# Giving z the 512-column products of q and k, and its silu in two parts

## The chip, the cores and the metric

The kernel runs on one core of one Trainium2 chip. The metric is the device time of one execution in microseconds (us), as the median of three runs. Below, PE is the matmul engine (TensorE), PEld its weight loads, DVE is VectorE, ACT is ScalarE, POOL is GpSimd, and SP is the engine that issues the large loads.

## What is computed

One layer of a hybrid decoder on 256 tokens of width 1024: a SwiGLU block, then a mixer with two branches side by side (a Mamba-2 state-space branch, "SSD", and differential attention), then a second SwiGLU block, each with a normalisation before and after. The part that matters here is the mixer's input projection and what hangs on its output `z`:

```python
u = rmsnorm(h, mix_pre_g[l])
z, xbc, dt_raw, q, k, v, gate_logits = jnp.split(u @ w_in[l], IN_SPLITS, axis=-1)
...
y = ssd_chunked(xh, dt, a_head, bm, cm)                      # the state-space recurrence, by chunks of 128
y = (y + d_skip[:, None] * xh)
y = y.reshape(b, L, SSD_D_INNER) * jax.nn.silu(z)            # z: 256 tokens x 2048
y = rmsnorm(y.reshape(b, L, SSD_GROUPS, ...), 1.0) * norm_g
return y @ w_branch
```

z has 2048 columns and q and k have 1024 each. Everything is float32, and the result has to be close to float32.

## The kernel before

**Products in parts.** Every weight and every activation is split into a high and a low float32r part (`whi`/`wlo`, and `uh`/`ul` for the normalised input u), and a product is the sum of high x high, high x low and low x high. The weights come as chunks of 1 MB: SP loads a chunk into one of three `raw` buffers, ACT casts its halves to `whi` (L250), and DVE subtracts to get `wlo` (L253). `take()` hands out the next chunk and first splits the chunks up to three ahead, so that two casts and two subtractions go with every chunk.

**Two ways of multiplying a chunk of 256 weight columns** with all 256 tokens, over eight blocks of 128 in the contraction:

- `mm_t` (L294) makes 48 products of 256 columns: per half of the chunk (`m`), 8 times `whi` x `uh` (L301), 8 times `whi` x `ul` (L302) and 8 times `wlo` x `uh` (L304). All three kinds add up in the same place, so that one buffer of PSUM holds both halves of the chunk. The weights `whi` are loaded twice.
- `mm_w` (L306) makes 32 products: per half, 8 products of `whi` with `uh` and `ul` side by side, 512 columns wide (L316), and 8 of `wlo` x `uh`, 256 columns wide (L315, L318). A half fills a whole buffer: its first 256 columns hold the part with `uh` and its last 256 the part with `ul`. ACT copies the second part to SBUF (L320, or L323 with a scale) and DVE adds the first (L321, or L324).

In both, the buffers are those of the pool `pj`, of which there are three. The kernel before uses `mm_w` for the gate and up products of both SwiGLU blocks and for q and k, and `mm_t` for the convolution's inputs (xs, B and C) and for z.

**The stage around the change.** After the eight chunks of xs come eight chunks of z (L1326 to L1332): each takes its weights, multiplies with `mm_t`, and ACT copies the 512 columns of the buffer to `sz` (L1331). After z follow q and k, alternately, in four chunks each: q0, k0, q1, k1, and so on.

**Work in the background.** `back.run(us)` stands behind every chunk. It issues steps of a background queue worth so many planned microseconds: `BG_US` = 3.15 behind a chunk of z and `QK_US` = 2.4 behind one of q or k. The queue holds `ssd_work` for four groups of eight heads. A group transposes xs (PE `px`, L1061; DVE multiplies to `X`, L1062), builds four decay tiles `E` (ACT L362 and DVE L1078 write parts, ACT takes the exponential, DVE multiplies by `cbm`, L1083), multiplies them (32 products into `py`, L1093) and adds to xs (DVE, L1100). The products begin with the group's last E. Behind it comes `ssd_norm`, which multiplies xs by silu(z) (DVE, L1107), squares, and normalises.

**silu(z).** After the last chunk of z, `act_table(SILU)` loads ACT's table for silu, four activations of 1024 columns apply silu to `sz`, and `act_table(EXP_LN)` loads the table of exponential and logarithm again. Only then is `ssd_norm` put in the queue. `act_table` also keeps activations on their side of the load.

**Order.** In this stage the order of instructions on each engine is the framework's: it plans them when the kernel is built, and the chip keeps each engine's order to the letter. A wait of one instruction holds up all that stand behind it on that engine. From the gates on (`pgt`), PE's order is as written.

Of the kernel before, what the change touches and what calls it, by code (L numbers as in the profile page):

```python
# [18 lines left out]
AF = mybir.ActivationFunctionType  # L19
# [4 lines left out]
EXP_LN = "natural_log_exp_and_others"  # L24
# [16 lines left out]
WARM = 3  # L41
FILL = 2
TAIL = 3
BG_US = 3.15
QK_US = 2.4
GATE_US = 1.75
SSD_US = 1.55
DOWN = {"f1": "p q1 p p q2 p ppp", "f2": "q1 p q2 p q3 ppp"}
# [5 lines left out]
def tile_hybrid_layer(ctx: ExitStack, tc: tile.TileContext, x, ffn1_pre_g, ffn1_w_gate, ffn1_w_up,  # L54
# [4 lines left out]
    nc = tc.nc  # L59
# [5 lines left out]
    def k4(shape, name, dt=F32):  # L65
        return sb.tile(shape, dt, tag="k4", name=name, bufs=K4_BUFS)
# [4 lines left out]
    def k2(shape, name, dt=F32):  # L71
        return sb.tile(shape, dt, tag="k2", name=name, bufs=K2_BUFS)
# [7 lines left out]
    def pj(name):  # L80

        return ps.tile([P, 512], F32, tag="pj", name=name, bufs=3)

    def pjt(name):

        return pj(name).rearrange("p (m t) -> p m t", m=2)

    def bg(shape, name):
        return ps.tile(shape, F32, tag="bg", name=name, bufs=5)
# [3 lines left out]
    class Quad:  # L93
# [32 lines left out]
        def split(self, p):  # L126
            load_to(self.i + 2)
            hi = k4([P, 2, 512], f"wqh{self.i}{p}", F32R)
            src = self.quarter(self.PLAIN[p], p) if p in self.PLAIN else self.sum_of(p)
            nc.scalar.copy(hi, src)  # L130
            for later in self.products[self.products.index(p) + 1:][:1]:
                if later in self.SUMS:
                    self.sum_of(later)
            lo = k4([P, 2, 512], f"wql{self.i}{p}", F32R)
            last_lo[0] = nc.vector.tensor_sub(lo, src, hi.bitcast(F32)).ins
            self.give_back()
            return lambda kt: hi[:, kt, :], lambda kt: lo[:, kt, :]
# [121 lines left out]
    def split_to(n):  # L259

        while len(splits) < min(n, len(units)):
            of, p = units[len(splits)]
            if p is not None:
                splits.append(of.split(p))
                continue
            for _ in split_steps():
                pass

    def ahead_of(i, n):

        n *= 4
        while n > 0 and i < len(units):
            n -= 4 if units[i][1] is None else 1
            i += 1
        return i

    def take(ahead=AHEAD):

        i = taken[0]
        taken[0] += 1  # L280
        split_to(ahead_of(i, ahead))
        (of, p), w = units[i], splits[i]
        splits[i] = None
        if p is not None:
            return w
        his, los = w
        nj = chunks[of][1][1] // 2
        return (lambda j: his[j // nj][:, j % nj, :], lambda j: los[j // nj][:, j % nj, :])
# [5 lines left out]
    def mm_t(acc, w, act, k0=0, first=True, last=True, ks=range(KD)):  # L294

        (wh, wl), (ah, al, _) = w, act
        acc = acc if isinstance(acc, list) else [acc[:, m, :] for m in range(2)]
        for m in range(2):
            cs = slice(m * P, (m + 1) * P)
            for j in ks:  # L300
                nc.tensor.matmul(acc[m], wh(j)[:, cs], ah(k0 + j), start=first and j == ks[0], stop=False)  # L301
                nc.tensor.matmul(acc[m], wh(j)[:, cs], al(k0 + j), start=False, stop=False)  # L302
            for j in ks:
                nc.tensor.matmul(acc[m], wl(j)[:, cs], ah(k0 + j), start=False, stop=last and j == ks[-1])  # L304

    def mm_w(dst, name, w, act, scale=None):  # L306


        (wh, wl), (ah, _, ahl) = w, act
        for m in range(2):  # L310
            acc = pj(f"{name}{m}")
            cs = slice(m * P, (m + 1) * P)
            for j in range(KD):
                if j:
                    nc.tensor.matmul(acc[:, :T], wl(j)[:, cs], ah(j), start=False, stop=False)  # L315
                nc.tensor.matmul(acc, wh(j)[:, cs], ahl(j), start=j == 0, stop=j == KD - 1)  # L316
                if not j:
                    nc.tensor.matmul(acc[:, :T], wl(j)[:, cs], ah(j), start=False, stop=False)  # L318
            if scale is None:
                nc.scalar.copy(dst[:, m, :], acc[:, T:])  # L320
                nc.vector.tensor_tensor(dst[:, m, :], acc[:, :T], dst[:, m, :], ALU.add)  # L321
            else:
                nc.scalar.activation(dst[:, m, :], acc[:, T:], AF.Copy, scale=scale)  # L323
                nc.vector.scalar_tensor_tensor(dst[:, m, :], acc[:, :T], scale, dst[:, m, :], ALU.mult, ALU.add)  # L324
# [29 lines left out]
    def act_table(name):  # L354
        f = nc.scalar.preload_act_table_set(name)
        for prev in act_since:
            tc.add_manual_dep(f.ins, prev, order, reason="activation table")
        act_since.clear()
        act_fence[0] = f.ins.name

    def act(*args, **kw):
        a = nc.scalar.activation(*args, **kw)  # L362
        if act_fence[0] is not None:
            tc.add_manual_dep(a.ins, act_fence[0], order, reason="activation table")
        act_since.append(a.ins.name)
# [65 lines left out]
    def new_u(tag):  # L431
        for i in range(2):
            uT[i] = sb.tile([P, 4, 2, T], F32R, tag="u8", name=f"u{i}_{tag}", bufs=2)

    act_u = (lambda j: uT[j // 4][:, j % 4, 0, :], lambda j: uT[j // 4][:, j % 4, 1, :],
             lambda j: uT[j // 4][:, j % 4, :, :])
# [594 lines left out]
    for i in range(4):  # L1031
        acc = pjt(f"pbc{i}")
# [18 lines left out]
    sz = [None] * 4  # L1051
# [52 lines left out]
    def ssd_norm(groups):  # L1104

        def one(g):
            nc.vector.tensor_tensor(xs[g], xs[g], sz[g], ALU.mult)  # L1107
            sq = k4([P, 4, T], f"sqy{g}")
            nc.scalar.activation(sq, xs[g], AF.Square)
            yield 1.2  # L1110
            nc.vector.tensor_tensor(sq[:, 0:2, :], sq[:, 0:2, :], sq[:, 2:4, :], ALU.add)
            nc.vector.tensor_tensor(sq[:, 0, :], sq[:, 0, :], sq[:, 1, :], ALU.add)
            ssum = k2([P, 2, T], f"ssum{g}", F32R)
            split(ssum[:, 0, :], ssum[:, 1, :], sq[:, 0, :])
            yield 1.5
            yield BREAK
            pn = bg([P, T], f"pn{g}")
            for i in range(2):
                nc.tensor.matmul(pn, ones_r, ssum[:, i, :], start=i == 0, stop=i == 1)
            rs = sq[:, 1, :]  # L1120
            act(rs, pn, AF.Ln, scale=1.0 / 512, bias=eps_c)
            act(rs, rs, AF.Exp, scale=-0.5)
            yield 0.1
            for c in range(4):
                n = col["ng"] + g * 4 + c
                nc.vector.scalar_tensor_tensor(xs[g][:, c, :], xs[g][:, c, :], cols_a[:, n:n + 1], rs,
                                               ALU.mult, ALU.mult)
            yh[g] = k4([P, 4, T], f"yh{g}", F32R)
            yl[g] = k4([P, 4, T], f"yl{g}", F32R)
            split(yh[g], yl[g], xs[g])  # L1130
            xs[g] = sz[g] = None
            yield 2.8

        todo = [one(g) for g in groups]
        under_way = []
        while todo or under_way:
            if todo and len(under_way) < 2:
                under_way.append(todo.pop(0))
            for w in list(under_way):
                us = next(w, None)  # L1140
                if us is None:
                    under_way.remove(w)
                else:
                    yield us
# [170 lines left out]
    back = Background()  # L1315
    back.add(cb_work())
    for g in range(4):
        xs[g] = k4([P, 4, T], f"xs{g}")
        for i in range(2):
            acc = pjt(f"pxs{g}{i}")  # L1320
# [5 lines left out]
    for g in range(4):  # L1326
        sz[g] = k4([P, 4, T], f"sz{g}")
        for i in range(2):
            acc = pjt(f"pz{g}{i}")
            mm_t(acc, take(), act_u)  # L1330
            nc.scalar.copy(sz[g][:, i * 2:i * 2 + 2, :], acc)  # L1331
            back.run(BG_US)  # L1332
    act_table(SILU)
    for g in range(4):
        act(sz[g], sz[g], AF.Silu)
    act_table(EXP_LN)
    back.add(ssd_norm(range(4)))
    for c in range(4):
        if c % 2 == 0:
            qT[c // 2] = k4([P, 4, T], f"q{c}")  # L1340
            kT[c // 2] = k4([P, 4, T], f"k{c}")
        o = (c % 2) * 2
        mm_w(qT[c // 2][:, o:o + 2, :], f"pq{c}", take(), act_u, 0.125)
        back.run(QK_US)
        mm_w(kT[c // 2][:, o:o + 2, :], f"pk{c}", take(), act_u)
        back.run(QK_US)

# [81 lines left out]
    acc = [[bg([P, 512], f"acc_mx{b}{q}") for q in range(2)] for b in range(2)]  # L1429
# [47 lines left out]
```

## Time and profile before

| what | value |
| --- | --- |
| median of 3 runs | 738.33 us (738.31 to 738.46) |
| the profiled execution | 737.54 us, of which its span is 735.8 us |
| PE busy | 726.4 us (99%), 4211 products |
| DVE busy | 591.9 us (80%) |
| ACT busy | 462.1 us (63%) |
| granted clock of PE | 0.997 of full speed |

Times in the profile's rows are counted from the span's start. A row of the timeline gives the start, the duration, the engine, the line, the operation, what is written and read, its shape, how many instructions are merged, and in brackets how long the engine sat idle before it and for whom. PE's products overlap: what a product costs is the distance from its start to the start of the next, not its own duration.

### The profile page before, as it was taken

To read this page: it belongs to the slowest core of one execution; us is meant where nothing else is said; L and a number is where in the kernel's file an instruction comes from. 1 tells how busy PE (TensorE), PEld (TensorE's weight loads), DVE (VectorE), ACT (ScalarE), POOL (GpSimd) and SP (SyncE) were. 2 spreads that over 40 slices of the span, in tenths; PEclk is the share of its full clock that TensorE was granted. 3 is DMA by queue.
4 is the path that set the end of the run, shared out by engine and by line. 5 is a ranking of instruction groups with operands and counts; after the bars stand their busy time and mean duration, and the time that the engine had idled before them with its cause. 6 is when DMAs were issued, how large, how long until landed. Compare 5 with 4: busy or idle time off the path is not lost.

```text
span 735.8 us, 10869 instructions
## 1 busy us (share of the span) xinstructions
PE 726.4 (99%) x4211; PEld 628.1 (85%) x4211; DVE 591.9 (80%) x904; ACT 462.1 (63%) x777; POOL 38.6 (5%) x72
## 2 busy tenths in 40 slices
PE   8999999999999999999999999999999999999996
PEld 6888888888889999999888788888888888888874
DVE  7978768998677878787996998785784878779994
ACT  7657556665566565958975577782663657566562
POOL 2700000000300000000000000000010000000000
PEclk9999999999999999999999999999999999999998
DMA  8884674469353647567464664475470765664541
GB/s 299 229 261 150 218 229 171 155 216 348 118 172 117 201 143 226 192 188 226 146 219 154 202 222 138 152 238 191 127 241 34 229 199 153 222 217 143 188 168 57
DMA packets 94212, 137.96 MB, mean 187 GB/s; under 512 B 2684, under 2 KB 68304, under 8 KB 94160
## 3 DMA queue, kind: packets, MB, share of 16 engines
q1 hardware_dynamic: 91488, 129.51, 54.2%
q0 software_dynamic: 2368, 7.22, 3.1%
q8 instruction: 33, 0.54, 0.3%
q10 hardware_dynamic: 304, 0.53, 0.2%
q14 instruction: 19, 0.16, 0.1%
HBM read 136.17 MB, written 1.08 MB: 187 GB/s over the span
## 4 chain that ended last, share of the span: by engine, by line
PE 97%; DVE 2%; issue 1%; DMA 0%; ACT 0%; DVEq 0%
PE pup_f L316 9%; PE pg_f L316 9%; PE pgt L335 6%; PE pws L335 6%; PE acc_f1p L625 5%; PE acc_f2p L625 4%; PE pg_f L315 4%; PE pup_f L315 4%; PE pn_f L335 3%; PE pn_mx L335 3%; PE acc_mx L573 3%; PE pn_f L345 3%; PE pwd L335 3%; PE acc_f1p L573 3%; PE pz L302 2%; PE pxs L304 2%
## 5 line engine op out<-in xcount | busy, mean ns | idle before, releaser
L253 DVE TENSOR_TENSOR wlo<-raw,whi 128x1024 fp32r<-128x1024 f32 (+1 forms) x226 | 266.6, 1208 | 22.7 <-ACT whi L250 21.7
L250 ACT CAST whi<-raw 128x1024 fp32r<-128x1024 f32 (+1 forms) x225 | 226.2, 1044 | 18.1 <-DMA raw<-in_w_in_dram 3.8
L316 PE MATMUL pup_f<-u_f,whi 128*128 128x512 f32 x288 | 101.3, 396 | 0.0
L316 PE MATMUL pg_f<-u_f,whi 128*128 128x512 f32 x288 | 101.2, 396 | 0.0
L315 PE MATMUL pg_f<-u_f,wlo 128*128 128x256 f32 x252 | 70.6, 280 | 0.0
L315 PE MATMUL pup_f<-u_f,wlo 128*128 128x256 f32 x252 | 70.3, 279 | 0.0
L316 PEld LDWEIGHTS pup_f<-u_f,whi 128*128 128x128 f32 x288 | 52.8, 188 | 9.8
L316 PEld LDWEIGHTS pg_f<-u_f,whi 128*128 128x128 f32 x288 | 52.8, 188 | 9.6
L315 PEld LDWEIGHTS pg_f<-u_f,wlo 128*128 128x128 f32 x252 | 47.5, 188 | 1.7
L315 PEld LDWEIGHTS pup_f<-u_f,wlo 128*128 128x128 f32 x252 | 47.5, 189 | 1.6
L321 DVE TENSOR_TENSOR su_f<-pup_f,su_f 128x256 f32<-128x256 f32 x36 | 15.1, 420 | 26.0 <-ACT su_f L320 25.8
L130 ACT CAST wqh<-wt 128x1024 fp32r<-128x1024 f32 x20 | 21.0, 1052 | 23.2 <-DVE wt L122 23.2
L320 ACT COPY su_f<-pup_f 128x256 f32<-128x256 f32 x36 | 13.4, 373 | 35.1 <-PE pup_f L316 34.9
L335 PE MATMUL pgt<-whi,u_mx 128*128 128x512 f32 x128 | 33.1, 393 | 0.0
L301 PE MATMUL pxs<-u_mx,whi 128*128 128x256 f32 x128 | 31.7, 285 | 0.0
L302 PE MATMUL pz<-u_mx,whi 128*128 128x256 f32 x128 | 31.6, 284 | 0.0
L301 PE MATMUL pz<-u_mx,whi 128*128 128x256 f32 x128 | 31.6, 284 | 0.0
L302 PE MATMUL pxs<-u_mx,whi 128*128 128x256 f32 x128 | 31.4, 283 | 0.0
L335 PEld LDWEIGHTS pgt<-whi,u_mx 128*128 128x128 f32 x128 | 23.6, 188 | 5.4 <-issue 0.7
L1009 DVE SCALAR_TENSOR_TENSOR xs<-pxs,cols_b,xs 128x255 f32<-128x255 f32 (+2 forms) x48 | 21.9, 475 | 6.3 <-ACT xs L1006 5.9
L291 ACT CAST gh_f<-sg_f 128x512 fp32r<-128x512 f32 x18 | 11.2, 622 | 21.5 <-DVE sg_f L771 21.5
L302 PEld LDWEIGHTS pz<-u_mx,whi 128*128 128x128 f32 x128 | 24.5, 192 | 0.2 <-issue 0.2
(397 smaller groups left out, 1698.5 us busy)
## 6 DMA issues: line engine op xcount, KB each, us to landing
raw<-in_w_in_dram SPq DMA_DIRECT2D x40, 1024.0 KB, 5.4
raw<-in_ffn_w_down_dram SPq DMA_DIRECT2D x22, 1024.0 KB, 4.9
raw<-in_ffn_w_gate_dram SPq DMA_DIRECT2D x20, 1024.0 KB, 5.6
raw<-in_ffn_w_up_dram SPq DMA_DIRECT2D x20, 1024.0 KB, 5.4
raw<-in_ssd_w_branch_dram SPq DMA_DIRECT2D x8, 1024.0 KB, 5.3
acb<-acd POOLq DMA_DIRECT2D x8, 512.0 KB, 5.5
raw<-in_da_w_branch_dram SPq DMA_DIRECT2D x4, 1024.0 KB, 5.1
raw<-in_w_out_dram SPq DMA_DIRECT2D x4, 1024.0 KB, 5.0
```

The lines of the kernel that those rows point to most:

```text
L130: nc.scalar.copy(hi, src)
L250: copy(hi[:, js, :], r[:, q * nj + j:q * nj + j + n, :])
L253: nc.vector.tensor_sub(lo[:, js, :], r[:, q * nj + j:q * nj + j + n, :], hi[:, js, :].bitcast(F32))
L301: nc.tensor.matmul(acc[m], wh(j)[:, cs], ah(k0 + j), start=first and j == ks[0], stop=False)
L302: nc.tensor.matmul(acc[m], wh(j)[:, cs], al(k0 + j), start=False, stop=False)
L315: nc.tensor.matmul(acc[:, :T], wl(j)[:, cs], ah(j), start=False, stop=False)
L316: nc.tensor.matmul(acc, wh(j)[:, cs], ahl(j), start=j == 0, stop=j == KD - 1)
L335: nc.tensor.matmul(acc, a(k0 + j), b(j), start=first and i == 0, stop=last and i == 11)
L345: nc.tensor.matmul(accs[b], x_(k0 + j), w_(j), start=first and j == 0 and w_ is wh and x_ is acts[b][0], stop=last and j == 3 and w_ is wl)
L573: nc.tensor.matmul(acc[b][q], x_[:, ts], w_(kt)[:, halves[q]], start=begin and i == 0 and kt == 0 and x_ is ah and w_ is wh, stop=i == n - ...
L625: nc.tensor.matmul(bank[p], x_, w_, start=p not in begun, stop=last and p in (1, 5, 6, 7))
L1009: nc.vector.scalar_tensor_tensor(dst[:, m, s:], acc[:, m, :T - s], cw(3 - s, c), dst[:, m, s:], ALU.mult, ALU.add)
```

## The change

z is multiplied with `mm_w`, so that ACT copies and DVE adds twice per chunk, each 256 columns wide. silu is applied to z's groups 0 and 1 before the first chunk of q, and to groups 2 and 3 behind the copies of that chunk; the second table load and `ssd_norm` move behind that too. The planned background is now 2.7 us behind a chunk of z and 2.8 us behind one of q or k.

```diff
-BG_US = 3.15
-QK_US = 2.4
+BG_US = 2.7
+QK_US = 2.8
...
         for i in range(2):
-            acc = pjt(f"pz{g}{i}")
-            mm_t(acc, take(), act_u)
-            nc.scalar.copy(sz[g][:, i * 2:i * 2 + 2, :], acc)
+            mm_w(sz[g][:, i * 2:i * 2 + 2, :], f"pz{g}{i}", take(), act_u)
             back.run(BG_US)
+    def gates_of_z(groups):
+        for g in groups:
+            act(sz[g], sz[g], AF.Silu)
+
     act_table(SILU)
-    for g in range(4):
-        act(sz[g], sz[g], AF.Silu)
-    act_table(EXP_LN)
-    back.add(ssd_norm(range(4)))
+    gates_of_z((0, 1))
     for c in range(4):
...
         mm_w(qT[c // 2][:, o:o + 2, :], f"pq{c}", take(), act_u, 0.125)
+        if c == 0:
+
+            gates_of_z((2, 3))
+            act_table(EXP_LN)
+            back.add(ssd_norm(range(4)))
         back.run(QK_US)
         mm_w(kT[c // 2][:, o:o + 2, :], f"pk{c}", take(), act_u)
         back.run(QK_US)
```

## The prediction

> **What bounds the kernel now.** I read the page first: the share of each engine, then the chain that ended last.
>
> ```profile
> span 735.8 us, 10869 instructions
> PE 726.4 (99%) x4211; PEld 628.1 (85%) x4211; DVE 591.9 (80%) x904; ACT 462.1 (63%) x777; POOL 38.6 (5%) x72
> ...
> PE 97%; DVE 2%; issue 1%; DMA 0%; ACT 0%; DVEq 0%
> ```
>
> PE is busy all the time and the chain runs through it. A busy PE could still hide waits, since its products overlap, so I read its waits next, and then the two stages that change, z and q/k, in the view by windows (its columns are the window's length, then the busy time of PE, PEld, DVE, ACT and POOL).
>
> ```profile
> PE warm L411 <- POOL ident L397: 1.6, 1, 1.6
> PE pn_f L345 <- DVE raw_u L464: 0.3, 1, 0.3
> PE pn_f L345 <- DVE whi L250: 0.3, 1, 0.3
> PE pu_f L456 <- DMA h<-in_x_dram: 0.2, 1, 0.2
> ```
>
> ```profile
> 289.28:343.87 54.59, 54.57 (x474) 52.73 (x473) 42.86 (x73) 40.32 (x82) 2.65 (x6) 1.00 0.65 203
> 343.87:394.90 51.03, 51.03 (x328) 43.49 (x327) 44.28 (x69) 39.09 (x70) 1.57 (x3) 1.00 0.68 217
> ```
>
> All four waits belong to the first block; in z and q/k PE waits for nobody, at full clock. So two things count: how much shorter PE's own work gets, and whether PE begins to wait. DVE is the engine to watch: 42.9 of 54.6 us in z, and 44.3 of 51.0 us (87%) in q/k.
>
> **PE's own work.** A chunk of z before, and one of q:
>
> ```profile
> 289.28 0.28 PE L301 MATMUL pz<-u_mx,whi 128*128 128x256 f32 x1
> 295.04 1.03 PE L1061 MATMUL px<-ident,xs 128*128 128x128 f32 x8
> ...
> 359.09 0.28 PE L318 MATMUL pq<-u_mx,wlo 128*128 128x256 f32 x1
> 361.91 0.28 PE L318 MATMUL pq<-u_mx,wlo 128*128 128x256 f32 x1
> 364.68 0.28 PE L318 MATMUL pk<-u_mx,wlo 128*128 128x256 f32 x1
> ```
>
> The first chunk of z takes 295.04 − 289.28 = 5.76 us for 48 products, 120 ns each. L318 is the second product of every half chunk in `mm_w`: the halves of q1 take 2.82 and 2.77 us, the chunk 5.59. Eight chunks save 8 × (5.76 − 5.59) = 1.36 us. Between 1.1 and 1.6 is all that the rows allow, as 0.03 us either way on a chunk is what the two halves differ by. The columns streamed are as many as before (48 × 256 = 16 × 512 + 16 × 256); only sixteen starts per chunk go.
>
> The Trainium skill speaks against even this: "TensorE: Matmul & The Clock Gate", section "Back-to-back issue gap", gives a warm gap of N/2.4 + 2.5 ns, which is 109 ns at 256 columns and 216 at 512, and a saving of 0.04 us a chunk, 0.3 us in all (an estimate from the page). The rows decide: they have 120 ns at 256 where all products are narrow, and q1 as measured.
>
> **What ACT and DVE get.** Sixteen copies of 256 columns take the place of eight of 512, and sixteen adds are new on DVE. They are off PE's path only as long as PE gets its buffers: there are three, each half of a chunk fills one, so a half waits until DVE has added the third half before it. The rows around the end of z carry the walk; I call the time at which PE has done z and starts q0 "E0" (343.87 here).
>
> ```profile
> 343.87 0.40 PE L316 MATMUL pq<-u_mx,whi 128*128 128x512 f32 x1
> 344.07 0.59 ACT L1331 COPY sz<-pz 128x512 f32<-128x512 f32 x1
> 344.55 1.28 ACT L362 ACTIVATE E<-acb,acs 128x128 f32<-128x128 f32 x4
> 345.74 0.62 ACT L362 ACTIVATE E<-E 128x512 f32<-128x512 f32 x1
> 346.38 1.28 ACT L355 ACT_TABLE_LOAD   x1
> 346.39 0.96 DVE L1083 TENSOR_TENSOR E<-E,cbm 128x768 f32<-128x768 f32 x1 [0.85 <-ACT E L362]
> 347.67 3.90 ACT L362 ACTIVATE sz<-sz 128x1024 f32<-128x1024 f32 x4
> 347.82 2.82 PE L1093 MATMUL py<-E,X 128*64 128x256 f32 x32
> 348.76 1.23 DVE L1107 TENSOR_TENSOR xs<-xs,sz 128x1024 f32<-128x1024 f32 x1 [1.41 <-ACT sz L362]
> 349.90 1.66 DVE L1100 SCALAR_TENSOR_TENSOR xs<-xs,cols_b,py 128x256 f32<-128x256 f32 x4
> 350.57 0.39 PE L315 MATMUL pq<-u_mx,wlo 128*128 128x256 f32 x1
> 351.48 2.35 DVE L1107 TENSOR_TENSOR xs<-xs,sz 128x1024 f32<-128x1024 f32 x2
> 351.58 1.28 ACT L355 ACT_TABLE_LOAD   x1
> 352.42 1.04 PE L1061 MATMUL px<-ident,xs 128*128 128x128 f32 x8
> 352.87 1.05 ACT L250 CAST whi<-raw 128x1024 fp32r<-128x1024 f32 x1
> 353.21 0.47 PE L316 MATMUL pk<-u_mx,whi 128*128 128x512 f32 x1
> 353.83 0.65 ACT L323 ACTIVATE q<-pq 128x256 f32<-128x256 f32 x2
> 353.95 1.23 DVE L253 TENSOR_TENSOR wlo<-raw,whi 128x1024 fp32r<-128x1024 f32 x1
> 355.10 0.75 DVE L324 SCALAR_TENSOR_TENSOR q<-pq,q 128x256 f32<-128x256 f32 x2
> 355.76 1.28 DVE L1062 TENSOR_TENSOR X<-px,dt 128x512 f32<-128x512 f32 x2
> 356.31 0.28 PE L318 MATMUL pk<-u_mx,wlo 128*128 128x256 f32 x1
> 356.96 2.35 DVE L253 TENSOR_TENSOR wlo<-raw,whi 128x1024 fp32r<-128x1024 f32 x2
> 359.23 0.47 DVE L1078 TENSOR_SCALAR E<-acb,acs 128x128 f32<-128x128 f32 x2
> 359.62 0.41 DVE L321 TENSOR_TENSOR k<-pk,k 128x256 f32<-128x256 f32 x1
> 359.95 0.47 DVE L1078 TENSOR_SCALAR E<-acb,acs 128x128 f32<-128x128 f32 x2
> ```
>
> Before, k0's second half starts at about 356.1 (its second product is the row at 356.31) and needs q0's first half off its buffer; DVE has that done at about 355.5 (the first of the two at 355.10), 0.6 us ahead. The cover was PE's own background between them: `py` (347.82 to 350.57, 2.75 us) and `px` (352.42 to 353.21, 0.79 us) stand inside q0.
>
> **First wait: k0's second half.** The order of instructions of the changed kernel has q0 and k0 whole, one behind the other; the `py` and `px` of that group come inside q1. So PE gets to k0's second half after three halves, at E0 + 3 × 2.8 = 8.4. What must be done by then, in the changed order on ACT from E0 + 0.20 (344.07 − 343.87): the last copy of z 0.27 (half of the two at 353.83 to the cast behind them), two parts of E 0.60 (half of 344.55 to 345.74), an exponential 0.6, four parts 1.19, an exponential 0.64: the table load begins at 3.5 and silu at 4.8 (1.29, from 346.38 to 347.67). DVE's first L1107 starts 1.09 behind the start of silu (348.76 − 347.67): 5.9. In its order stand two L1107 (1.13 each, from the pair of 2.35), a `wlo` (1.15, from 353.95 to 355.10) and only then the add of q0's first half (0.42): 5.9 + 2.26 + 1.15 + 0.42 = 9.7. ACT's copy of it is ready by then: after two silus, a cast, and a third silu, 4.8 + 4 × 0.97 + 0.3 = 9.0. PE waits from 8.4 to 9.75, **1.3 us**. Moving only two silus behind q0 does not help, for the third and the cast still stand ahead of the copy; what it saves is the second table load (1.29) ahead of it.
>
> **Second wait: q2's second half.** After the table is changed back, ACT makes the group's last E: 9.0 + 0.27 (q0's second copy) + 0.97 (fourth silu) + 1.29 + 1.19 + 0.62 = 13.3, and DVE multiplies it by 14.2 (0.87 to 0.96). From there DVE is without a gap until the add of k1's first half, which frees the buffer for q2's second half. Its order has six `wlo` at 1.13 (6.8), four L1100 (1.6), five adds at 0.33 (1.65; from 359.62 to 359.95), two L1062 (1.2), eight L1078 at 0.195 (1.6), three L1083 at 0.87 (2.6) and one L1107 (1.1): 16.5, done at 30.8. PE, having left its first wait at 9.75, comes there after six halves, a `py` and a `px`: 9.75 + 16.8 + 3.54 = 30.1. It waits another **0.7 us**, 2.0 in all. How large the first wait is hardly matters for this total: the second is set by the table loads and DVE's row, so if PE passed the first free, it would stand at the second for all 2.0.
>
> **The rest costs nothing by the same walk.** I followed z in the same way, with these durations and the changed order, and give the outcome as estimates. The tightest places are the `py` of the first two groups, where DVE's last E ends within 0.2 us of PE's arrival, on either side. Buffers come free 2 to 4 us early, except one (for z2's second half) with 0.1. SP's loads and POOL's `acb` transfers are issued in the same sequence as before and are wanted more than 2 us after they land. If this cover is gone, each late add in z costs PE what it is late. Past k2 DVE has fewer steps and catches up; a PE that comes 2 us later finds it further ahead.
>
> **Sum.** −1.36 + 2.0 = +0.65, say +0.7 us on the profiled execution: 737.5 to 738.2. The profiled execution lies 0.8 below the median of the runs, so the median goes from 738.3 to **739.0**. What a measurement of this kernel can tell from no change is about 0.2%, 1.5 us; this lies within it.
>
> **The rivals.**
>
> *No wait.* ACT and DVE keep up, and only PE's saving is left: −1.1 to −1.6, 736.7 to 737.2. For it: PE waits for nothing in q/k now, with DVE at 87%. Against: the cover of 3.54 us between q0 and k0 moves behind k0, and the slack there is 0.6. With half the waits it is 737.9. Chance 0.25 for none or nearly none; in 0.08 the gain passes 0.2%, which needs the upper end of the saving.
>
> *Slower: DVE becomes the bound of all of q/k.* The planned background moves from z to q/k: 8 × 0.4 = 3.2 us more there, on an engine with 44.28 busy and 6.75 idle of 51.03. If that idle time is what its fixed order costs whatever its load (waits for copies and exponentials), the stage takes 54.2 us, 3.2 more. Minus the saving of 1.36 that is +1.9, 740.2; with the first wait on top (1.3) it is 741.5. It decides once DVE is later than three halves (8.4 us) behind PE for more than one half in a row. For it: z's adds are new heads of queue on which DVE waits for PE. Against: by the walk only two adds are late. Chance 0.22.
>
> *The wide product is no faster.* If one of 512 columns cost two of 256 (240 ns), nothing is saved and 2.0 is lost: 740.3. The rows of q1 speak against it. Chance 0.03. With the saving that the Trainium skill's gap gives (0.3, above) it would be 740.0.
>
> *The edit does not do what it says.* The planner could set all four silus ahead of q0's copies as before. Its order shows three ahead and one behind; this is already in the walk.
>
> **Chances.** The forecast has 0.5 (737.9 to 739.8: two waits of 1.0 to 2.8 in all). Faster by over 0.2% 0.08; slower by over 0.2% is the second and third rival, less their milder part, and the forecast's far end: 0.28; within 0.2% the remaining 0.64. The range from 736.9 to 740.9 leaves out the last of each end.
>
> **What would show it.** In the profile after: z's window about 53.2 us long; PE waits for DVE `q` L324 (about 1.3) at k0 and for DVE `k` L321 (about 0.7) at q2, in the list of PE's waits. Wrong would be: no such waits (then the first rival), waits at many halves of q and k (the second), or a z window not shorter than 54 (the third).

## The result, and the profile after

| kernel | median (us) | lowest to highest | ratio to before, 95% interval |
| --- | --- | --- | --- |
| before | 738.34 of 18 runs | 737.71 to 740.9 | |
| after | 739.68 of 18 runs | 738.88 to 741.2 | 1.0016 [1.0008, 1.0023] |

By the ratio the changed kernel is 1.2 us slower (0.0016 × 738.34; 0.6 to 1.7 by the interval). That is a small loss, but zero lies outside the interval. The prediction said 739.0, and its range of 736.9 to 740.9 contains the measured 739.68.

The page of the changed kernel: the shares of the engines, and the chain that ended last.

```profile
span 738.7 us, 10624 instructions
PE 727.3 (98%) x4083; PEld 621.7 (84%) x4083; DVE 596.6 (81%) x920; ACT 462.2 (63%) x785; POOL 38.6 (5%) x72
...
PE 87%; DVE 5%; ACT 3%; DMA 2%; issue 2%; POOL 0%; SPq 0%; DVEq 0%; ACTq 0%; POOLq 0%
```

128 products are gone (4211 to 4083), DVE has sixteen more instructions and ACT eight. The chain, 97% PE before, is 87% PE now, with 5% DVE and 3% ACT: it leaves PE where PE waits. PE's waits in the changed kernel say where (total, times, longest):

```profile
PE pk L316 <- DVE q L324: 1.1, 1, 1.1
PE pu_mx L456 <- DVE h L550: 0.6, 1, 0.6
PE pq L316 <- DVE k L321: 0.6, 1, 0.6
```

The first and the last line are new and lie in q/k: k0's second half and q2's second half. The one between them is not in the list of before either, but it lies in the block ahead of z, which the change does not touch.

For lengths I measure z from its first product to q0's first, and q/k from there to the first product of the gates. The prediction's window of q/k ended 0.96 us earlier, so this is before's row for the longer one. The columns are the window, its length, the busy time of PE, PEld, DVE, ACT and POOL with their counts, the granted clock, the DMA share and GB/s:

```profile
343.87:395.86 51.99, 51.99 (x334) 44.34 (x333) 44.95 (x70) 39.13 (x71) 1.57 (x3) 1.00 0.67 213
```

And the two stages after; the third window is the stretch that ends with the second wait:

```profile
290.86:344.32 53.46, 53.46 (x346) 45.58 (x345) 45.52 (x82) 38.27 (x82) 2.64 (x5) 1.00 0.68 208
344.32:398.50 54.18, 52.53 (x333) 44.32 (x332) 47.19 (x77) 41.84 (x79) 1.59 (x3) 1.00 0.63 197
358.50:375.28 16.78, 16.33 (x112) 13.49 (x110) 16.78 (x30) 13.48 (x32) 0.00 (x0) 1.00 0.53 157
```

z fell by 1.13 (54.59 to 53.46) and q/k rose by 2.19 (51.99 to 54.18): +1.06 together. The spans of the two profiled executions differ by 2.9 (738.7 and 735.8), but 1.58 of that lies ahead of z, which starts at 290.86 against 289.28. That code is the same in both, and most of the 1.58 does not come back when the same kernel is profiled again (below, `after_again`). What belongs to the change is the 1.06, which agrees with the 1.2 of the ratio.

The timeline of the changed kernel around the two waits (start, duration, engine, line, operation, idle time before in brackets). E0, where q0 starts, is 344.32:

```profile
347.72 1.28 ACT L355 ACT_TABLE_LOAD   x1
349.01 2.01 ACT L362 ACTIVATE sz<-sz 128x1024 f32<-128x1024 f32 x2
350.11 2.36 DVE L1107 TENSOR_TENSOR xs<-xs,sz 128x1024 f32<-128x1024 f32 x2 [1.42 <-ACT sz L362]
350.93 1.04 ACT L250 CAST whi<-raw 128x1024 fp32r<-128x1024 f32 x1
351.87 1.05 ACT L362 ACTIVATE sz<-sz 128x1024 f32<-128x1024 f32 x1
352.39 1.22 DVE L253 TENSOR_TENSOR wlo<-raw,whi 128x1024 fp32r<-128x1024 f32 x1
352.50 0.40 PE L316 MATMUL pk<-u_mx,whi 128*128 128x512 f32 x1
352.82 0.63 ACT L323 ACTIVATE q<-pq 128x256 f32<-128x256 f32 x2
353.52 0.75 DVE L324 SCALAR_TENSOR_TENSOR q<-pq,q 128x256 f32<-128x256 f32 x2
353.99 0.50 PE L316 MATMUL pk<-u_mx,whi 128*128 128x512 f32 x1 [1.10 <-DVE q L324]
357.54 0.96 DVE L1083 TENSOR_TENSOR E<-E,cbm 128x768 f32<-128x768 f32 x1 [3.27 <-ACT E L362]
374.43 0.40 PE L316 MATMUL pq<-u_mx,whi 128*128 128x512 f32 x1
374.91 0.75 DVE L321 TENSOR_TENSOR k<-pk,k 128x256 f32<-128x256 f32 x2
375.38 0.50 PE L316 MATMUL pq<-u_mx,whi 128*128 128x512 f32 x1 [0.55 <-DVE k L321]
375.72 0.28 PE L318 MATMUL pq<-u_mx,wlo 128*128 128x256 f32 x1
```

The chain of the first wait can be read off in order: table load, silu, two multiplications on DVE, a `wlo`, and then the add of q0's first half at 353.52, behind which PE goes on at 353.99. For the second, DVE first sits idle for 3.27 us until ACT, late by the table loads, has the group's last E (357.54). From 358.50 on, the third window above shows DVE busy for 16.78 of 16.78 us up to the end of the add of k1's first half, which starts at 374.91: from there on DVE alone holds PE.

The idle time in brackets is less than what a wait costs. The last product ahead of the first wait starts at 352.50 and is drawn 0.40 long, but a wide product without a wait has its successor 0.23 us behind its start. PE could have gone on at 352.73 and went on at 353.99: 1.26 us are lost there. In the same way 0.72 are lost at the second wait (374.43 + 0.23, to 375.38). The first product behind a wait takes 0.34 to the next (375.38 to 375.72) instead of 0.23, so each wait costs 0.11 more. Together that is 2.20, and q/k grew by 2.19.

### The profile page after: what moved, and what is told of

The parts are those of the page before. It is cut to its first block, busy times and chain, and to the rows that moved or that the text cites. A ratio compares the mean times of both kernels' runs of the same rounds, so it can differ in the third digit from the quotient of the medians.

```text
span 738.7 us, 10624 instructions
## 1 busy us (share of the span) xinstructions
PE 727.3 (98%) x4083; PEld 621.7 (84%) x4083; DVE 596.6 (81%) x920; ACT 462.2 (63%) x785; POOL 38.6 (5%) x72
## 4 chain that ended last, share of the span: by engine, by line
PE 87%; DVE 5%; ACT 3%; DMA 2%; issue 2%; POOL 0%; SPq 0%; DVEq 0%; ACTq 0%; POOLq 0%
PE pup_f L316 9%; PE pg_f L316 9%; PE pws L335 6%; PE pgt L335 6%; PE pz L316 4%; PE pg_f L315 4%; PE pup_f L315 4%; PE acc_f2p L625 3%; PE acc_f1p L625 3%; PE pn_f L345 3%; PE pn_f L335 3%; PE pn_mx L335 3%; PE acc_mx L573 3%; PE pwd L335 3%; DVE wlo L253 2%; PE pxs L304 2%
## 5 line engine op out<-in xcount | busy, mean ns | idle before, releaser
L316 PE MATMUL pz<-u_mx,whi 128*128 128x512 f32 x128 | 45.1, 400 | 0.0
L315 PE MATMUL pz<-u_mx,wlo 128*128 128x256 f32 x112 | 31.4, 280 | 0.0
```

## The experiments

My theory was that of the prediction, made sharper by the order of PE's instructions. The new amounts of planned background take the third group's `py` and `px` out of q0. With that cover gone, q0's add is late: on ACT its copy stands behind the table load and silu, and the add stands behind what DVE does with their result. The rival was the wide z itself: DVE gets sixteen adds more, comes late out of z, and drags that into q/k. The three edits of the change (wide z, silu in two parts, new amounts) can be made one by one.

### z_only: the wide product alone

```diff
-            acc = pjt(f"pz{g}{i}")
-            mm_t(acc, take(), act_u)
-            nc.scalar.copy(sz[g][:, i * 2:i * 2 + 2, :], acc)
+            mm_w(sz[g][:, i * 2:i * 2 + 2, :], f"pz{g}{i}", take(), act_u)
```

> z in products of 512 columns alone; planned amounts (3.15 and 2.4) and the whole silu block in front of q as before. The order of instructions has the third group's py between q0's halves again. Theory (the table and silu block without cover makes the waits): PE wants k0's second half at E0 + 11.9, q0's first add is done at about 11.6, so the waits at k0 and q2 are gone or under 0.3 us; z's products save about 1.1 to 1.3; with 3.15 planned behind a chunk and the new adds, DVE may be 0 to 2 us late for the second group's py in z. From z's first product to the gates' first: 1.2 shorter than before, to 0.8 longer. Rival (z's adds alone make DVE late): the same two waits, about 1.7 us, and the stretch 0.5 to 1 us longer than before.

Measured: 737.31 against 737.98, ratio 0.9988 [0.9977, 0.9999]. Its windows of z and of q/k, and its only wait of PE there:

```profile
290.39:344.42 54.03, 53.67 (x347) 45.55 (x346) 47.31 (x87) 40.36 (x91) 2.62 (x5) 1.00 0.66 205
344.42:396.42 52.00, 52.00 (x334) 44.39 (x333) 45.68 (x72) 39.37 (x70) 1.58 (x3) 1.00 0.68 213
```

```profile
PE pz L316 <- DVE sz L321: 0.4, 1, 0.4
```

z is 0.56 shorter and q/k as long as before (52.00 and 51.99). The wide z with its sixteen adds by itself delays nothing in q/k: as the cause of the two waits, the rival falls. With the old amounts z itself has one wait of 0.4, for a buffer that DVE empties late.

### z_split: wide z and silu in two parts, with the old amounts

The changed kernel with two constants put back:

```diff
-BG_US = 2.7
-QK_US = 2.8
+BG_US = 3.15
+QK_US = 2.4
```

> The change with the planned amounts of before (3.15 and 2.4): z wide and the silu in two parts. py stands between q0's halves. Theory: q0's first add is done at E0 + 10.8, PE wants the buffer at 11.9: no wait at k0 or q2; the same open place in z as without the split, 0 to 2 us at the second py. Stretch from z to the gates 1.2 shorter to 0.8 longer than before. Rival (z's adds): two waits, 1.7 us.

Measured: 737.57, ratio 0.9992 [0.9981, 1.0003]; z and q/k:

```profile
289.41:343.43 54.02, 53.66 (x347) 45.56 (x345) 47.30 (x87) 40.35 (x91) 2.63 (x5) 1.00 0.66 205
343.43:395.51 52.08, 52.08 (x334) 44.33 (x333) 45.51 (x72) 39.50 (x70) 1.58 (x3) 1.00 0.68 213
```

Splitting silu neither helps nor harms here (−0.01 and +0.08 against `z_only`), and both waits of the changed kernel are gone. So the two constants hold them.

### plan_only: the new amounts alone

The kernel before with nothing but the two constants of the change:

```diff
-BG_US = 3.15
-QK_US = 2.4
+BG_US = 2.7
+QK_US = 2.8
```

> The planned amounts of the change (2.7 and 2.8) alone; z narrow, silu whole in front of q. The order has q0 whole and the third group's py four products into k0's second half. Theory: PE wants k0's second half at E0 + 8.4; ACT has a table, four silus, a table and a cast ahead of q0's copy, DVE a wlo ahead of the add: done at about 12.0, a wait of 3.6 us; the q2 wait does not follow since PE is then late enough. Stretch 3 to 4 us longer than before, median about 742. Rival (z's adds are the cause): no wait, since there are none; stretch as before.

Measured: 744.25, ratio 1.0076 [1.0047, 1.0106]. PE's new wait, the rows of PE's timeline that follow it, and the windows of z, of q/k and of the time around the wait:

```profile
PE pk L316 <- DVE q L324: 3.6, 1, 3.6
```

```profile
356.13 0.80 PE L316 MATMUL pk<-u_mx,whi 128*128 128x512 f32 x1 [3.63 <-DVE q L324]
357.77 4.69 PE L1093 MATMUL py<-E,X 128*64 128x256 f32 x32
```

```profile
289.30:343.93 54.63, 54.61 (x475) 52.78 (x473) 41.38 (x68) 38.31 (x76) 2.63 (x5) 1.00 0.67 206
343.93:402.47 58.54, 54.91 (x334) 45.96 (x333) 46.93 (x75) 41.33 (x76) 1.59 (x3) 0.94 0.59 186
...
351.37:354.78 3.41, 1.13 (x7) 0.71 (x5) 0.58 (x2) 3.39 (x5) 0.00 (x0) 1.00 0.43 144
354.78:361.61 6.83, 5.47 (x28) 3.75 (x30) 6.13 (x9) 4.09 (x10) 0.00 (x0) 0.50 0.61 163
```

With narrow products in z, and DVE 41.38 busy there instead of 45.52, PE waits at the same place, and longer: 3.6, for here all four silus and the second table load stand ahead of q0's copies. The place, the engine and the size of the wait were as the theory has them. The stretch was not: 3 to 4 us were expected, and +6.55 in q/k (58.54 − 51.99) is 2.9 more than the wait. Nearly all of that is the clock: from 354.78 to 361.61 PE was granted half (0.50), and `py` took 4.69 us instead of 2.82. PE was busy for 5.47 us in that window, which at full clock would have been about half (an estimate), so some 2.7 us go to the clock and the rest to the start of the wait, as above. I had not expected that at all.

### z_plan: wide z and the new amounts, silu whole

The edit of `z_only` and that of `plan_only` together.

> The change without the split: z wide, new planned amounts, the whole silu block in front of q. Theory: q0's first add done at about E0 + 12.5, wanted at 8.4: a wait of 4.1 us at k0's second half, none at q2; with z's saving of 1.1 the stretch is 3.0 us longer than before, median about 741.3. So the split is worth about 2 us where the planned amounts are the new ones. Rival (z's adds): the same 1.7 us as the change, whatever the split.

Measured: 743.05, ratio 1.0066 [1.0044, 1.0088].

```profile
PE pk L316 <- DVE q L324: 4.0, 1, 4.0
```

```profile
289.49:342.95 53.46, 53.46 (x346) 45.59 (x345) 45.53 (x82) 38.24 (x82) 2.62 (x5) 1.00 0.68 208
342.95:400.73 57.78, 53.77 (x333) 45.21 (x332) 47.83 (x77) 41.77 (x79) 1.58 (x3) 0.97 0.59 190
...
351.78:355.19 3.41, 0.00 (x0) 0.00 (x0) 1.27 (x2) 3.40 (x7) 0.00 (x0) 1.00 0.03 12
355.19:358.60 3.41, 3.07 (x14) 2.10 (x16) 3.07 (x5) 3.08 (x6) 0.00 (x0) 0.50 0.67 181
```

Three things follow. z is as short as in the changed kernel (53.46), so the new amounts do help z: 0.57 over `z_only`, the wait of 0.4 and 0.2 of PE's own time. Splitting silu is worth much once the amounts are new: 3.6 us in q/k (57.78 to 54.18). And the long wait has its price in clock again: 57.78 is 5.79 over before, 1.8 more than the wait of 4.0. PE was granted half for 3.41 us, 3.07 of them busy, which is some 1.5 us of the 1.8 by the same estimate. The wait was as long as expected, and because of the clock the stretch grew by more than the 3.0 expected: z and q/k take 4.66 us more than before (111.24 against 106.58).

### split_plan: the changed kernel with narrow products in z

```diff
-            mm_w(sz[g][:, i * 2:i * 2 + 2, :], f"pz{g}{i}", take(), act_u)
+            acc = pjt(f"pz{g}{i}")
+            mm_t(acc, take(), act_u)
+            nc.scalar.copy(sz[g][:, i * 2:i * 2 + 2, :], acc)
```

> The change without its wide products: z narrow as before, the split of silu and the new planned amounts. The order around q0 and k0 is that of the change. Theory (the waits are those of the table and silu block without cover): ACT reaches the table load at E0 + 3.1, q0's first add is done at 9.25, wanted at 8.4: a wait of about 0.9 at k0's second half; the chain to k1's first add ends at 30.2, wanted at 29.7: 0.5 at q2's second half. Stretch from z to the gates 1.4 to 1.8 us longer than before, z itself no shorter. Rival (z's adds make DVE late): no waits, stretch as before.

Measured: 739.96, ratio 1.002 [1.0011, 1.003].

```profile
PE pk L316 <- DVE q L324: 0.7, 1, 0.7
PE pq L316 <- DVE k L321: 0.5, 1, 0.5
```

```profile
289.56:344.18 54.62, 54.60 (x475) 52.76 (x474) 41.37 (x68) 38.31 (x76) 2.64 (x5) 1.00 0.67 207
344.18:398.00 53.82, 52.55 (x335) 44.33 (x334) 46.11 (x75) 41.39 (x76) 1.58 (x3) 1.00 0.62 195
```

Both waits are there without the wide z. z and q/k take 1.86 more than before (108.44 against 106.58), a little more than the 1.4 to 1.8 expected. So of the loss of 2.19 in q/k the wide z has 0.36 (54.18 − 53.82), and the amounts with the split silu have 1.83. The 0.36 can be followed on ACT:

```profile
347.20 1.28 ACT L355 ACT_TABLE_LOAD   x1
```

The first table load starts 3.02 behind q0's start here (344.18) and 3.40 behind it in the changed kernel (347.72 − 344.32), where ACT comes out of z with more parts of E still to do. All that follows is earlier by as much: PE leaves the first wait at E0 + 9.29 instead of 9.67 and the second at E0 + 30.68 instead of 31.06.

### gates_after_k0: the whole silu block behind k0

If the block in front of q0's copies is the cause, it need only stand elsewhere. Here wide z and the new amounts stay; nothing is left in front of q0:

```diff
-    act_table(SILU)
-    gates_of_z((0, 1))
     for c in range(4):
...
         mm_w(qT[c // 2][:, o:o + 2, :], f"pq{c}", take(), act_u, 0.125)
-        if c == 0:
-            gates_of_z((2, 3))
-            act_table(EXP_LN)
-            back.add(ssd_norm(range(4)))
         back.run(QK_US)
         mm_w(kT[c // 2][:, o:o + 2, :], f"pk{c}", take(), act_u)
+        if c == 0:
+            act_table(SILU)
+            gates_of_z(range(4))
+            act_table(EXP_LN)
+            back.add(ssd_norm(range(4)))
         back.run(QK_US)
```

> The change with the same wide z and the same planned amounts, but the whole silu block (table, four silus, table) and the adding of ssd_norm behind k0 instead of around q0. The order has the third group's py and px within k0. Theory: q0's copies stand ahead of the table on ACT, q0's adds are done by E0 + 7, k0's second half finds its buffer free; k0's first add is done at about 13, wanted at 17.5; no waits of over 0.3 us. Stretch 1.1 us shorter than before (2.2 shorter than the change), median about 737.2. Rival (new planned amounts overload DVE in q and k, whatever the block): waits of 1 us or more in q and k remain, stretch no shorter than before.

Measured: 737.08 against 738.17, ratio 0.9985 [0.9976, 0.9995]. z and q/k, then ACT's copies and table load, DVE's add of q0's first half and PE's `py`:

```profile
290.05:343.49 53.44, 53.44 (x346) 45.59 (x345) 45.50 (x82) 38.24 (x82) 2.63 (x5) 1.00 0.68 208
343.49:395.53 52.04, 52.04 (x333) 44.29 (x332) 47.42 (x77) 41.78 (x79) 1.58 (x3) 1.00 0.67 211
```

```profile
348.02 0.36 ACT L323 ACTIVATE q<-pq 128x256 f32<-128x256 f32 x1
348.99 0.42 DVE L324 SCALAR_TENSOR_TENSOR q<-pq,q 128x256 f32<-128x256 f32 x1
349.29 0.38 ACT L323 ACTIVATE q<-pq 128x256 f32<-128x256 f32 x1
351.15 1.28 ACT L355 ACT_TABLE_LOAD   x1
351.41 2.82 PE L1093 MATMUL py<-E,X 128*64 128x256 f32 x32
```

PE waits nowhere in z or q/k. q0's halves are copied at 348.02 and 349.29, 4.5 and 5.8 us behind q0's start, ahead of the table load. The stretch is 105.48 against 106.58, 1.10 shorter: all of the saving in z arrives. The order of this kernel also has `py` inside k0's first half (351.41), so k0's second half has cover again, as the expectation says. It does not need it: q0's first add is done at E0 + 5.92 (349.41), and without cover PE wants the buffer at E0 + 8.4. DVE is as loaded in q/k as in the changed kernel (47.42 and 47.19), so its load alone was not what made PE wait; the order was. This version is faster than before by 1.1 us (0.4 to 1.8 by the interval), and its median of 737.08 is 2.2 below the changed kernel's (739.28, `after_again`).

### after_again: the changed kernel once more

> The change itself once more, for a second profile: 1.6 us of the first one's span were lost ahead of z, in code that is the same in both. Both theories: z about 53.5 us, waits of 1.1 and 0.6 us at k0 and q2, stretch 1.1 us longer than before; the 1.6 us ahead of z do not come back in the same way.

Measured: 739.28 against 738.17, ratio 1.0014 [1.0003, 1.0025].

```profile
289.59:343.05 53.46, 53.46 (x346) 45.59 (x345) 45.52 (x82) 38.24 (x82) 2.63 (x5) 1.00 0.68 208
343.05:397.24 54.19, 52.55 (x333) 44.33 (x332) 47.16 (x77) 41.82 (x79) 1.58 (x3) 1.00 0.62 196
```

The lengths of the two stages repeat within 0.01 us. The time ahead of z does not: 289.59 here, 290.86 in the first profile. Over the nine profiles it lies between 289.28 and 290.86, in code that is the same in all. What differs there between two executions of one kernel stays open; it is not the change.

## Why the prediction was right, point by point

| step | predicted | measured |
| --- | --- | --- |
| z's products | −1.36 (1.1 to 1.6) | −1.13 |
| k0's second half | waits 1.3, goes on at E0 + 9.75 | loses 1.26 (idle 1.10), goes on at E0 + 9.67 |
| q2's second half | waits 0.7, goes on at E0 + 30.8 | loses 0.72 (idle 0.55), goes on at E0 + 31.06 |
| q/k in all | +2.0 | +2.19 |
| z and q/k | +0.65 | +1.06 |
| median | +0.7 | +1.2 by the ratio |

The prediction counted a wait from the time at which PE could have gone on, so it is the lost time that compares with its figures. The profiled execution took 740.38, not the 738.2 of the sum: 1.58 of that lies ahead of z, where nothing was changed. The median does not have this.

**z's products.** The sum's largest term was 0.23 too big, near the lower end of its bounds. It was taken from undisturbed half chunks of q1, 2.8 us each. In z the eight chunks are also cut by three `px` and two `py`, and the products around a cut run further apart. PE's timeline of the changed kernel, in z's first chunks and behind one of these `px`:

```profile
290.86 0.40 PE L316 MATMUL pz<-u_mx,whi 128*128 128x512 f32 x1
291.09 0.28 PE L318 MATMUL pz<-u_mx,wlo 128*128 128x256 f32 x1
...
318.05 0.48 PE L316 MATMUL pz<-u_mx,whi 128*128 128x512 f32 x1
318.36 0.28 PE L318 MATMUL pz<-u_mx,wlo 128*128 128x256 f32 x1
```

A wide product takes 0.23 from its start to the next (291.09 − 290.86), and 0.31 behind a `px` (318.36 − 318.05). Counted by PE's starts over the whole stage, z's own products take 46.66 us before, where eight undisturbed chunks would be 8 × 5.76 = 46.08, and 45.67 after, where they would be 8 × 5.59 = 44.72. So what undisturbed chunks leave out is 0.58 before and 0.95 after, most of it in halves next to a `px` or `py`. The `px` give 0.14 back (2.43 to 2.29). 0.95 − 0.58 − 0.14 is the missing 0.23: the sum set this term at nothing.

A saving of only 0.3, as the gap in "TensorE: Matmul & The Clock Gate" would have it (the Trainium skill, section "Back-to-back issue gap"), the trace does not bear out: it has 1.13. That section of the Trainium skill gives this gap for a single product by itself and says that in a stream of weight loads and products both set the distance, so the prediction took it too strictly as a rule for z.

**The first wait.** The walk by ACT's and DVE's orders gave the place, the add waited for and the time to 0.1 us. That the lost cover of `py` and `px` is the condition was argued then. It is shown now: the three kernels with that cover in q0 (before, `z_only`, `z_split`) and the one with the block away from q0's copies (`gates_after_k0`) do not wait there, and the four others do (after, `plan_only`, `z_plan`, `split_plan`). What the prediction did not say is which edit moves the cover: it is the two constants, not the wide z.

**The second wait.** It is DVE without a gap behind a late E, as written: DVE starts on the last E at E0 + 13.22 (357.54), against 13.3 in the walk, and then has 16.78 us of work up to the end of the add, against 16.5. The prediction also held that the total is set there, and that a shorter first wait would be made up at the second. No run tests that. In `split_plan` the first wait is 0.4 shorter and the second no longer, but there the table load itself is 0.38 earlier, and both waits end earlier by as much; this fits a total that is set by the table loads and DVE's row, without proving it.

**Nothing else.** In the changed kernel PE waits for nothing else in the two stages: not at a `py`, and at no half of z. For z that held with the new amounts only: with the old ones (`z_only`, `z_split`) a half of z waits 0.4 for its buffer.

**The rivals.** No wait in q/k is what the wide z gives without the new amounts, or with the silu block elsewhere. DVE as the bound of all of q/k is out: it is full for the 16.78 us up to the second wait, and PE waits at two halves in all and nowhere after the second. The wide product as no faster is out by z's 1.13.

## What to carry to other kernels

Before moving background work, ask what it stood in front of. Here 3.5 us of `py` and `px` on PE hid a block of table load and activations on ACT that stands ahead of the copies out of PE's three buffers. Such a block belongs behind the copies that the next product needs, not in front of them, as `gates_after_k0` shows. Walking each engine's order with durations from the trace found the late add to 0.1 us. A wait's idle time in the profile is not all that it costs: here 1.10 idle were 1.26 lost. And try the parts of an edit one by one: of three here, the wide product gains, the new amounts lose as long as the block stands where it does, and the split of silu mends part of that loss.

## What was not expected of the hardware

A wait of PE can cost more than its length. After the waits of 3.6 and 4.0 us the granted clock was one half for 6.83 us in `plan_only` (354.78 to 361.61) and for 3.41 us in `z_plan` (355.19 to 358.60), which made up most of the 2.9 and 1.8 us by which the stage grew beyond the wait. The waits of 1.1 and 0.6 us in the changed kernel left the clock at 1.00. Where between 1.1 and 3.6 us it starts was not tried. In `plan_only` the drop began at 354.78, before the wait's end at 356.13 and only 2.3 us behind its start at 352.50.

The Trainium skill, in "TensorE: Matmul & The Clock Gate", section "What's actually happening", tells of a gate that passes half or all of the clock, judged by windows of about 3.4 us that run on whatever the kernel does, and that falls to half after an idle window. The traces agree in the one half and in the two lengths, one window and two. In `z_plan` a window that ends where the clock falls would begin at 351.78, and PE is idle in all of it, as the Trainium skill has it. In `plan_only` it would begin at 351.37, and PE is busy in it for 1.13 of 3.41 us. If the windows do end where the clock falls, then, a window that is idle for two thirds can be enough.
